# Scores of three attention blocks: 64-row products per head, or 128-row products with q's two parts stacked

## The chip, the cores and the metric

The kernel runs on one core of a Trainium2 chip. Its time is the device time of one execution in microseconds, median of several executions on the same chip. The engines that matter here are TensorE (PE in the rows, PEld for its weight loads), VectorE (DVE), ScalarE (ACT), GpSimd (POOL, which here only issues DMAs), and SyncE (SP, which issues the loads of weights).

## What is computed

Two transformer blocks are applied to x of 512 tokens by 1024 features, all in float32. The parts that the change touches are three attention blocks. In the first block a windowed attention (a, 8 heads of 64, 2 heads of k and v, window 128) and a neighbourhood attention (b, 8 heads, each with its own k and v) are computed from the same normalised input; in each layer of the second block there is one sliding-window attention (c, 8 heads of q, 2 of k and v). Cut to what matters:

```python
sc = jnp.einsum('bqkgd,bskd->bkgqs', qi, ki).astype(jnp.float32) * scale
sc = sc - slopes[:, :, None, None] * dist.astype(jnp.float32)
sc = jnp.where(valid, sc, -jnp.inf)
p = jax.nn.softmax(jnp.concatenate([sc, sink_col], axis=-1), axis=-1)[..., :-1]
return jnp.einsum('bkgqs,bskd->bqkgd', p.astype(v.dtype), vi)
```

Around them stand the products with w_in, the gates, w_proj and w_out, and the feed-forward layers with w_up, w_down and the gated pairs, which take most of the time.

## The kernel before, in words

Activations are kept transposed, features on partitions and 512 tokens along the free axis. Each float32 operand is held as two float32r tiles, a high part (a rounded copy, made by ScalarE) and a low part (the rest, made by VectorE), and each product is three matmuls: high by high, high by low, low by high. The tiles live in 52 slots of 128 by 512 (`slot[i]`, named r in the rows); `take` and `give` hand them out.

`Tile.mm` (lines 460 to 462) makes a product of a weight block with the activations, 24 matmuls of 512 columns for 1024 features. Weights come through `raw` and are split by line 386 (ScalarE) and line 388 (VectorE), five half-blocks ahead of their use.

The products for q, k and v end in an evacuation: `scaled` (lines 863 and 865; `scaled_by_columns`, line 871, for b) multiplies by the norm's factor `inv` on VectorE into a tile `evs`, and `split_act` (lines 566 and 567) makes the high part on ScalarE and the low part on VectorE, each 128 by 512. One such tile holds two heads, head g = 0 on partitions 0 to 63 and g = 1 on 64 to 127.

An attention block is a list of steps, one for a pair of heads c and a block of 128 queries i: 16 steps each for a and b, in one run, and 16 for c in each layer. A step has four stages. `qk` makes the scores (line 734, tiles sa, sb, sc): for each of the two heads three matmuls that contract over the head's 64 partitions, over 256 or 384 keys; then VectorE adds the bias and takes the maximum (line 739) and the negated maximum (lines 744 to 749). `soft` takes the exponentials on ScalarE (lines 755 and 758) and returns `rest`, the division by the sum on VectorE (lines 763 to 766). `tr` transposes the probabilities on TensorE (line 775, tiles pt) and splits them (lines 566 and 567). `pv_` multiplies with v (line 795, tiles ya, yb, yc; 128 rows, 256 columns), and `y_plain` evacuates the result (lines 903 and 904) in two halves of 64 partitions.

`run_attention` writes out the order of the work by hand. It goes through turns s; in each it issues `qk` of step s, then fillers (the products for later q, k, v, gates and so on, in the order of the tables FILL_AB and FILL_C, in portions of six matmuls) up to the middle of the turn, then `pv_` and `tr` of earlier steps, then `soft` of step s, two weight splits, `rest`, and fillers again. `tr` comes one turn after `soft` in a and b and two turns after in c. With `head=1` two filler portions (12 matmuls) stand ahead of the first scores. What is issued is executed in that order on each engine. `ev_v` defers the transposes of v (tile vtr) to the end of a later product.

Tables of bias for b (bb) are loaded by DMAs that GpSimd issues; SyncE's queue carries the weights.

## Time and profile before

| | us |
|---|---|
| median of 3 runs (2461.2 to 2463.68) | 2461.51 |
| the profiled execution | 2462.84 |
| its span | 2461.0 |
| TensorE busy | 2438.8 (99%) |
| VectorE busy | 1959.3 (80%) |
| ScalarE busy | 1261.1 (51%) |
| GpSimd busy | 11.6 (0%) |
| attention a and b in the span | about 31 to 263 |
| attention c of each layer | about 1085 to 1190 and 1950 to 2055 |

The profile's page is read from above: busy time of each engine, the chain of work that ended last, and the groups of instructions by line. A matmul's recorded duration includes the way through the array, so two matmuls in a row overlap in the rows; what one costs is the distance from its start to the next one's start.

### The profile page before, as it was taken

How to read it: one execution, taken by the hardware profiler on the slowest of the kernel's cores; microseconds unless marked ns; L12 is line 12 of the kernel's file. 1: busy time of each engine (PE TensorE's matmuls, PEld its weight loads, DVE VectorE, ACT ScalarE, POOL GpSimd, SP SyncE). 2: the span in 40 equal slices, each digit the busy share in tenths (PEclk: the TensorE clock that was granted, in tenths of full speed). 3: DMA queues.
4: the chain of work that ended last, by engine and by line, in shares of the span. 5: the costliest groups of instructions: out<-in, count | busy, mean ns of one | idle time of the engine just before them, and what ended most of it. 6: DMA issues, size and time to landing. Idle time of an engine off the chain costs nothing.

```text
span 2461.0 us, 39533 instructions
## 1 busy us (share of the span) xinstructions
PE 2438.8 (99%) x15118; PEld 2171.3 (88%) x15118; DVE 1959.3 (80%) x3950; ACT 1261.1 (51%) x2744; POOL 11.6 (0%) x26
## 2 busy tenths in 40 slices
PE   9999999999999999999999999999999999999998
PEld 7888888999879999988899999899999878999997
DVE  7778578877689878768798888898887687988885
ACT  5554355544465545544565445665445454654454
POOL 0000000000000000000000000000000000000000
PEclk9999999999999999999999999999999999999999
DMA  4222332333323332322223333323333322233322
GB/s 162 70 93 90 121 108 82 101 95 103 105 83 99 96 112 87 114 95 69 86 82 99 108 98 102 103 93 110 99 104 107 102 69 77 75 107 107 107 94 80
DMA packets 74621, 239.45 MB, mean 97 GB/s; under 512 B 8768, under 2 KB 10816, under 8 KB 74432
## 3 DMA queue, kind: packets, MB, share of 16 engines
q1 hardware_dynamic: 71248, 228.49, 29.3%
q0 software_dynamic: 1600, 6.82, 1.0%
q8 instruction: 118, 1.93, 0.3%
q10 hardware_dynamic: 1584, 1.64, 0.2%
q14 instruction: 71, 0.58, 0.1%
HBM read 234.81 MB, written 2.10 MB: 96 GB/s over the span
## 4 chain that ended last, share of the span: by engine, by line
PE 93%; DVE 5%; ACT 1%; issue 0%; DMA 0%; ACTq 0%; DVEq 0%
PE X L1114 7%; PE X L1112 7%; PE X L1113 7%; PE YZ L1112 5%; PE YZ L1113 5%; PE YZ L1114 5%; PE mlp_D L460 2%; PE mlp_D L461 2%; PE mlp_D L462 2%; PE 1, 'ffn1'_D L460 2%; PE 0, 'ffn2'_D L460 2%; PE 0, 'ffn1'_D L460 2%; PE 0, 'ffn2'_D L461 2%; PE 0, 'ffn1'_D L461 2%; PE 1, 'ffn1'_D L461 2%; PE 0, 'ffn1'_D L462 2%
## 5 line engine op out<-in xcount | busy, mean ns | idle before, releaser
L388 DVE TENSOR_TENSOR wl<-raw,wh 128x512 fp32r<-128x512 f32 (+2 forms) x890 | 531.8, 609 | 96.0 <-ACT wh L386 89.1
L386 ACT CAST wh<-raw 128x512 fp32r<-128x512 f32 (+2 forms) x890 | 469.8, 556 | 5.3 <-PE 0, 'ffn2'_D L461 1.0
L1112 PE MATMUL X<-r,wh 128*128 128x256 f32 x1568 | 445.2, 284 | 3.8 <-ACT g L1118 3.6
L1114 PE MATMUL X<-r,wl 128*128 128x256 f32 x1568 | 444.1, 283 | 0.0
L1113 PE MATMUL X<-r,wh 128*128 128x256 f32 x1568 | 443.9, 283 | 0.0
L386 ACT CAST wh<-s 128x512 fp32r<-128x512 f32 x392 | 242.6, 620 | 224.0 <-DVE s L365 218.7
L1112 PE MATMUL YZ<-r,wh 128*128 128x256 f32 x1176 | 334.2, 284 | 0.8 <-ACT u L1124 0.8
L1113 PE MATMUL YZ<-r,wh 128*128 128x256 f32 x1176 | 333.2, 283 | 0.0
L1114 PE MATMUL YZ<-r,wl 128*128 128x256 f32 x1176 | 333.1, 283 | 0.0
L388 DVE TENSOR_TENSOR wl<-s,wh 128x512 fp32r<-128x512 f32 x392 | 268.9, 686 | 69.2 <-ACT wh L386 67.4
L1112 PEld LDWEIGHTS X<-r,wh 128*128 128x128 f32 x1568 | 300.2, 191 | 15.2 <-ACT g L1118 4.0
L1113 PEld LDWEIGHTS X<-r,wh 128*128 128x128 f32 x1568 | 300.2, 191 | 10.3 <-issue 1.2
L1114 PEld LDWEIGHTS X<-r,wl 128*128 128x128 f32 x1568 | 300.3, 192 | 0.0
L1112 PEld LDWEIGHTS YZ<-r,wh 128*128 128x128 f32 x1176 | 226.2, 192 | 1.6 <-ACT u L1124 1.4
L1113 PEld LDWEIGHTS YZ<-r,wh 128*128 128x128 f32 x1176 | 226.1, 192 | 0.2 <-issue 0.2
L1114 PEld LDWEIGHTS YZ<-r,wl 128*128 128x128 f32 x1176 | 226.1, 192 | 0.0
L1126 ACT COPY g<-X 128x256 f32<-128x256 f32 x98 | 36.5, 372 | 141.6 <-PE X L1114 141.4
L1127 DVE TENSOR_TENSOR u<-u,g 128x256 f32<-128x256 f32 x98 | 41.6, 425 | 75.8 <-ACT g L1126 75.8
L460 PE MATMUL mlp_D<-r,wh 128*128 128x512 f32 x256 | 100.1, 391 | 0.0
L461 PE MATMUL mlp_D<-r,wh 128*128 128x512 f32 x256 | 100.1, 391 | 0.0
L462 PE MATMUL mlp_D<-r,wl 128*128 128x512 f32 x256 | 99.6, 389 | 0.0
L1122 ACT COPY u<-X 128x256 f32<-128x256 f32 x98 | 36.5, 373 | 101.0 <-PE X L1114 101.0
(426 smaller groups left out, 5251.2 us busy)
## 6 DMA issues: line engine op xcount, KB each, us to landing
raw<-in_w SPq DMA_DIRECT2D x318, 512.0 KB, 3.7
raw<-in_w SPq DMA_DIRECT2D x64, 384.0 KB, 3.4
raw<-in_w SPq DMA_DIRECT2D x32, 448.0 KB, 3.7
raw<-in_w SPq DMA_DIRECT2D x32, 320.0 KB, 2.9
raw<-in_w SPq DMA_DIRECT2D x32, 256.0 KB, 2.7
bb<-in_rpb POOLq DMA_DIRECT2D x12, 384.0 KB, 3.5
xt<-in_x POOLq DMA_DIRECT2D x8, 256.0 KB, 2.9
xt<-in_x SPq DMA_DIRECT2D x2, 512.0 KB, 6.3
```

Source lines behind the costliest of these rows:

```text
L386: nc.scalar.copy(h[:, :w], src)
L388: nc.vector.tensor_tensor(lo[:, :w], src, h[:, :w].bitcast(F32), ALU.subtract)
L460: nc.tensor.matmul(self.ps, h[:, c], hx, start=(self.n == 1), stop=False)
L461: nc.tensor.matmul(self.ps, h[:, c], lx, start=False, stop=False)
L462: nc.tensor.matmul(self.ps, lo[:, c], hx, start=False, stop=end)
L1112: nc.tensor.matmul(out, h[:, c], hx, start=first, stop=False, skip_group_check=skip)
L1113: nc.tensor.matmul(out, h[:, c], lx, start=False, stop=False, skip_group_check=skip)
L1114: nc.tensor.matmul(out, l[:, c], hx, start=False, stop=(k == 3), skip_group_check=skip)
L1122: nc.scalar.copy(u[:, lo], out)
L1126: nc.scalar.copy(g[:, hi], out)
L1127: nc.vector.tensor_tensor(u[:, hi], u[:, hi], g[:, hi], ALU.add)
```

## The change

The scores of a head are now made over all 128 partitions. For each head g a slot holds q's high part in the head's own 64 partitions and q's low part in the other 64. For k there are two slots for each head: one with k's high part in both halves, one with its low part in both. A score is then two matmuls, the stacked q with each of the two; together they also contain the product of the two low parts. `ev_q` and `ev_k` take the place of `ev_split`: the high and low parts are made by operations of 64 partitions each, and what has to stand in the other half is copied there by DMAs that GpSimd issues (`move`), two for each q and four for each k, of 64 by 512 elements. k takes four slots in place of two. k's product now stands ahead of q's at the head of each attention block and for each pair in FILL_AB, where the kb and qb entries also come earlier, and `head=2` puts 24 filler matmuls ahead of the first scores. In `run_attention` the exponentials (`soft`) are issued ahead of `pv_` and `tr`; `rest` stays where it was. In `y_plain` both high copies come ahead of both low parts.

```diff
-MIX1_HEAD = [("qa", 0), ("ka",), ("va",)]
+MIX1_HEAD = [("ka",), ("qa", 0), ("va",)]
...
             for g in range(2):
-                r = slice(HD * g, HD * g + HD)
-                qs = slice(P * i, P * i + P)
-                for j, (a, b) in enumerate(((qh, kh), (qh, kl), (ql, kh))):
-                    nc.tensor.matmul(sp[:, g, :w], a[r, qs], b[r, sl], start=(j == 0), stop=(j == 2))
+                qg, kg = slot[q(c)[g]], k(c)[2 * g:2 * g + 2]
+                for j in range(2):
+                    nc.tensor.matmul(sp[:, g, :w], qg[:, P * i:P * i + P], slot[kg[j]][:, sl], start=(j == 0), stop=(j == 1))
...
-    def run_attention(steps, fillers, needs, head=1, late=False):
+    def run_attention(steps, fillers, needs, head=2, late=False):
...
             fill_to((s + MID) / slots, SLACK[0])
+            if s < n:
+                rest = steps[s][1](steps[s][4])
             if s > lag:
                 k = s - lag - 1
                 steps[k][3](steps[k][4])
             if lag <= s < n + lag:
                 steps[s - lag][2](steps[s - lag][4])
             if s < n:
-                rest = steps[s][1](steps[s][4])
                 split_to(st["next"] + 2)
                 rest()
...
+    def rows(g):
+
+        return slice(HD * g, HD * g + HD)
+
+    def move(out, g_out, src, g_src):
+        nc.gpsimd.dma_start(out.bitcast(F32)[rows(g_out), :], src[rows(g_src), :])
+
+    def ev_q(ids, turn=scaled):
+
         def f(ps):
-            split_act(turn(ps, "evs", scale), slot[ids[0]], slot[ids[1]])
+            t = turn(ps, "evs", QS)
+            for g in range(2):
+                nc.scalar.copy(slot[ids[g]][rows(g), :], t[rows(g), :])
+            for g in range(2):
+                nc.vector.tensor_tensor(t[rows(g), :], t[rows(g), :], slot[ids[g]][rows(g), :].bitcast(F32), ALU.subtract)
+            for g in range(2):
+                move(slot[ids[g]], 1 - g, t, g)
+        return f
+
+    def ev_k(ids, turn=scaled):
+
+        def f(ps):
+            t = turn(ps, "evs")
+            for g in range(2):
+                nc.scalar.copy(slot[ids[2 * g]][rows(g), :], t[rows(g), :])
+            for g in range(2):
+                hi, lo = slot[ids[2 * g]], slot[ids[2 * g + 1]]
+                nc.vector.tensor_tensor(lo[rows(g), :], t[rows(g), :], hi[rows(g), :].bitcast(F32), ALU.subtract)
+            for j in range(2):
+                for g in range(2):
+                    i = ids[2 * g + j]
+                    move(slot[i], 1 - g, slot[i].bitcast(F32), g)
         return f
...
             for g in range(2):
                 r = slice(HD * g, HD * g + HD)
+                nc.scalar.copy(hi[r, cs].rearrange("p (a q) -> p a q", a=2), yp[r, :, g, :])
+            for g in range(2):
+                r = slice(HD * g, HD * g + HD)
                 src = yp[r, :, g, :]
-                nc.scalar.copy(hi[r, cs].rearrange("p (a q) -> p a q", a=2), src)
```

The order on the engines moves at three places. First, TensorE at the first scores of block a. Before (qa_388 is the product for the second pair of heads; after the arrow stand the streamed k, then the loaded q):

```order
L461 MATMUL qa_388<-r_95,wh_268 128x512
L462 MATMUL qa_388<-r_94,wl_269 128x512
L734 MATMUL sa_407<-r_106,r_104 128x256
L734 MATMUL sa_407<-r_107,r_104 128x256
L734 MATMUL sa_407<-r_106,r_105 128x256
```

The same three names follow for the second head, on the other 64 partitions, and then the second half of qa_388. After (qa_398 is the same product, vtr the transposes of v, qa_462 the next product):

```order
L462 MATMUL qa_398<-r_102,wl_322 128x512
L915 MATMUL vtr<-ident,evv 128x128 x4
L731 MATMUL sa_440<-r_106,r_104 128x256
L731 MATMUL sa_440<-r_107,r_104 128x256
L731 MATMUL sa_440<-r_108,r_105 128x256
L731 MATMUL sa_440<-r_109,r_105 128x256
L460 MATMUL qa_462<-r_88,wh_327 128x512
```

Six matmuls have become four, and all of qa_398 and the four transposes now stand ahead of them.

Second, ScalarE in a turn of block a. Before (ya is a product with v, pta the transposes of probabilities, mxa and ta the maxima and scores of the turn's own step, wh a weight split):

```order
L903 CAST r_116<-ya_557 64x256 x2
L566 CAST r_138<-pta_639 128x768
L755 ACTIVATE mxa_605<-mxa_605 128x2
L758 ACTIVATE ta_604,dena_649<-ta_604,mxa_605 128x256 x2
L386 CAST wh_662<-raw_335 128x512
```

After, in the same turn:

```order
L386 CAST wh_642<-raw_335 128x512
L752 ACTIVATE mxa_637<-mxa_637 128x2
L755 ACTIVATE ta_636,dena_653<-ta_636,mxa_637 128x256 x2
L929 CAST r_116<-ya_592 64x256 x2
L566 CAST r_138<-pta_669 128x768
```

The exponentials have moved ahead of the evacuations of the product and of the transposes.

Third, GpSimd ahead of the first scores of block b. Before (bb are the bias tables; nothing but the making of `ident` stands on this queue ahead of them):

```order
L945 MEMSET ident 128x128
L946 ISA
L946 AFFINE_SELECT ident<-ident 128x128
L1022 DMA bb_1545<-in_rpb 128x768
L1022 DMA bb_1549<-in_rpb 128x768
L1022 DMA bb_1621<-in_rpb 128x768
```

After (r_118 to r_129 are the slots of the second pair's k, r_130 one of its q's):

```order
L879 DMA r_118<-r_118 64x512
L879 DMA r_128<-r_128 64x512
L879 DMA r_119<-r_119 64x512
L879 DMA r_129<-r_129 64x512
L1051 DMA bb_1556<-in_rpb 128x768
L1051 DMA bb_1560<-in_rpb 128x768
L879 DMA r_130<-evs 64x512
```

The loads of the bias tables now stand behind the moves of k in GpSimd's queue.

## Rows read from the trace of the kernel before

**Rows 1.** Page, chain that ended last, share of the span by engine

```profile
PE 93%; DVE 5%; ACT 1%; issue 0%; DMA 0%; ACTq 0%; DVEq 0%
```

**Rows 2.** Busy time by stretch; columns: stretch, length, then busy (count) by engine

```profile
28.00:138.00 110.00, 109.27 (x605) 88.03 (x606) 83.89 (x239) 55.73 (x143) 1.21 (x2) 1.00 0.22 68
138.00:260.00 122.00, 121.46 (x678) 98.69 (x677) 96.13 (x251) 60.24 (x155) 5.37 (x10) 1.00 0.29 90
1080.00:1190.00 110.00, 110.00 (x592) 88.26 (x592) 87.97 (x264) 55.02 (x154) 0.00 (x0) 1.00 0.25 73
```

**Rows 3.** Timeline of PE, a score block of 256 keys; columns: start, duration, instruction

```profile
57.02 0.39 PE L462 MATMUL ga<-r,wl 128*128 128x512 f32 x1
57.34 0.62 PE L734 MATMUL sa<-r,r 64*128 64x256 f32 x6
...
58.23 0.40 PE L461 MATMUL ga<-r,wh 128*128 128x512 f32 x1
```

**Rows 4.** The same, only what runs at 57.36 to 57.45

```profile
57.34 0.39 PE L734 MATMUL sa<-r,r 64*128 64x256 f32 x2
```

**Rows 5.** The same view, a score block of 384 keys

```profile
37.06 0.40 PE L462 MATMUL qa<-r,wl 128*128 128x512 f32 x1
37.38 0.80 PE L734 MATMUL sa<-r,r 64*128 64x384 f32 x6
...
38.45 0.39 PE L461 MATMUL qa<-r,wh 128*128 128x512 f32 x1
```

**Rows 6.** The same view, a product with v in block a, 128 rows

```profile
59.18 0.39 PE L462 MATMUL ga<-r,wl 128*128 128x512 f32 x1
59.40 1.24 PE L795 MATMUL ya<-r,r 128*128 128x256 f32 x9
60.48 0.60 PE L775 MATMUL pta<-ident,ta 128*128 128x128 f32 x4
```

**Rows 7.** Timeline, all engines, start of block a

```profile
27.94 0.69 DVE L865 SCALAR_TENSOR_TENSOR evs<-qa,inv 128x512 f32<-128x512 f32 x1 [1.90 <-ACT inv L703]
28.66 0.62 ACT L566 CAST r<-evs 128x512 fp32r<-128x512 f32 x1 [0.76 <-DVE evs L865]
...
28.68 0.50 PE L460 MATMUL qa<-r,wh 128*128 128x512 f32 x1 [0.70 <-DVE evs L865]
...
31.61 1.05 PE L734 MATMUL sa<-r,r 64*128 64x256 f32 x6
```

**Rows 8.** DMA issues: count, KB each, median us from issue to landing

```profile
bb<-in_rpb POOLq DMA_DIRECT2D x12, 384.0 KB, 3.5
xt<-in_x POOLq DMA_DIRECT2D x8, 256.0 KB, 2.9
```

**Rows 9.** Groups by line: count | busy, mean ns | idle before, releaser

```profile
L1120 DVE TENSOR_TENSOR g<-YZ,g 128x256 f32<-128x256 f32 x98 | 40.8, 416 | 0.0
...
L904 DVE TENSOR_TENSOR r<-yc,r 64x256 fp32r<-64x256 f32 x32 | 13.5, 421 | 10.7 <-ACT r L903 10.3
```

**Rows 10.** Waits of VectorE, us 28 to 260; columns: total us, times, longest

```profile
DVE r L904 <- ACT r L903: 9.2, 17, 1.7
...
DVE dena L763 <- ACT ta L758: 5.2, 12, 0.6
```

**Rows 11.** The same, us 1080 to 1190

```profile
DVE r L904 <- ACT r L903: 4.4, 9, 1.0
DVE denc L763 <- ACT tc L758: 4.2, 11, 0.6
```

**Rows 12.** Waits of TensorE, us 28 to 260

```profile
PE qa L460 <- DVE evs L865: 0.7, 1, 0.7
```

**Rows 13.** Timeline, all engines, a late step of block a

```profile
129.36 0.75 DVE L766 TENSOR_SCALAR ta<-ta,dena 128x384 f32<-128x384 f32 x2
...
130.25 0.82 PE L775 MATMUL pta<-ident,ta 128*128 128x128 f32 x6
```

**Rows 14.** Timeline, all engines, start of block c

```profile
1078.64 0.59 ACT L703 COPY inv<-spread 128x512 f32<-128x512 f32 x1 [1.73 <-PE spread L691]
```

More of the change, by code (lines that the diff above doesn't have):

```diff
@@ L76 @@
 GB_ORDER += [("pb", 6), ("pb", 7)]
-MIX2_HEAD = [("q", 0), ("k",), ("v",)]
+MIX2_HEAD = [("k",), ("q", 0), ("v",)]
 FILL_C = [("q", 1), ("cc", 0), ("ch", 0), ("q", 2), ("cb", 0), ("cc", 1), ("ch", 1), ("q", 3), ("cc", 3),
@@ L725, in qk @@
             sp = bank(f"s{kind}{s}", True).rearrange("p (g k) -> p g k", g=2)
-            qh, ql = q(c)
-            kh, kl = k(c)
             w = max(n, 2 * P)
@@ L874, in scaled_by_columns @@
         return t
-    def ev_split(ids, scale=1.0, turn=scaled):
-        def f(ps):
-            split_act(turn(ps, "evs", scale), slot[ids[0]], slot[ids[1]])
+    def rows(g):
[3 more added lines that the diff above has]
+    def ev_q(ids, turn=scaled):
+        def f(ps):
+            t = turn(ps, "evs", QS)
[18 more added lines that the diff above has]
+                    move(slot[i], 1 - g, slot[i].bitcast(F32), g)
         return f
@@ L965, in two_blocks @@
     qa, ya, yb, qb, kb, vb = {0: take(2)}, {}, {}, {}, {}, {}
-    ka, va = take(2), take(2)
-    linear2(MIX1_HEAD, xop, [ev_split(qa[0], QS), ev_split(ka), ev_v(va)], ar, KC, make_inv, (5, 7))
+    ka, va = take(4), take(2)
+    linear2(MIX1_HEAD, xop, [ev_k(ka), ev_q(qa[0]), ev_v(va)], ar, KC, make_inv, (5, 7))
     ya_done = []
@@ L996, in make @@
                 return halves(key, [pair_of(ya[k]) for k in range(4)], ev_pa(key[1]))
-            ids = take(2)
+            ids = take(4 if key[0] == "kb" else 2)
             {"qa": qa, "qb": qb, "kb": kb, "vb": vb}[key[0]][key[1]] = ids
-            ev = {"qa": lambda: ev_split(ids, QS), "qb": lambda: ev_split(ids, QS, scaled_by_columns),
-                  "kb": lambda: ev_split(ids, 1.0, scaled_by_columns), "vb": lambda: ev_v(ids, scaled_by_columns)}
+            ev = {"qa": lambda: ev_q(ids), "qb": lambda: ev_q(ids, scaled_by_columns),
+                  "kb": lambda: ev_k(ids, scaled_by_columns), "vb": lambda: ev_v(ids, scaled_by_columns)}
             return halves(key, xop, ev[key[0]]())
@@ L1039, in rpb_bias @@
         return bt[:, :, P:] if i == 0 else bt
-    f_a = make_attention("a", ids_pair(qa), lambda c: pair_of(ka), lambda c: pair_of(va),
+    f_a = make_attention("a", qa.get, lambda c: ka, lambda c: pair_of(va),
                          y_plain(ya, lambda c: qa[c] + (ka + va if c == 3 else []), ya_done),
                          alibi("a", 0, 384), 0, (-1, 0, 1))
-    f_b = make_attention("b", ids_pair(qb), ids_pair(kb), ids_pair(vb),
+    f_b = make_attention("b", qb.get, kb.get, ids_pair(vb),
                          y_plain(yb, lambda c: qb[c] + kb[c] + vb[c]), rpb_bias, None, (-1, 0, 1))
@@ L1341, in mix2 @@
         qs, ys, tmp = {0: take(2)}, {}, {}
-        ks, vs = take(2), take(2)
-        linear2([(l,) + k for k in MIX2_HEAD], xop, [ev_split(qs[0], QS), ev_split(ks), ev_v(vs)], ar, 1, make_inv)
+        ks, vs = take(4), take(2)
+        linear2([(l,) + k for k in MIX2_HEAD], xop, [ev_k(ks), ev_q(qs[0]), ev_v(vs)], ar, 1, make_inv)
         cs = [take(2, late=True) for _ in range(4)]
@@ L1372, in make @@
                     qs[key[1]] = take(2)
-                    return halves((l,) + key, xop, ev_split(qs[key[1]], QS))
+                    return halves((l,) + key, xop, ev_q(qs[key[1]]))
                 return halves((l,) + key, xop, ev_conv(*key))
             return (key, 1.0, make)
-        f_c = make_attention(f"c{l}", ids_pair(qs), lambda c: pair_of(ks), lambda c: pair_of(vs),
+        f_c = make_attention(f"c{l}", qs.get, lambda c: ks, lambda c: pair_of(vs),
                              y_plain(ys, lambda c: qs[c] + (ks + vs if c == 3 else [])),
```

4 rows, old and new, of the table FILL_AB are left out of this document.

## The prediction

> **What bounds the kernel now.** I read the chain of waits first: 93% of the work that ended last is TensorE [rows 1]. Then the busy time by stretch over the three attention parts, the only places that the change reaches: TensorE is busy for 109.3 of 110 us and 121.5 of 122 in a and b, and for all of 110 in c [rows 2]; c comes once in each of two layers. TensorE waits for others almost nowhere: its largest wait in a and b is 0.7 us at the very start [rows 12]. So a TensorE slot that goes away shortens the run, as long as the engines beside it keep up. VectorE is the one to watch: busy for 83.9 + 96.1 = 180 of 232 us in a and b and for 88 of 110 in c [rows 2], and part of its idle time is waiting for ScalarE [rows 10, 11].
>
> **The scores, before.** Six matmuls look like six slots, but they aren't. A look at a moment inside the block shows two of them at once: the pair takes 0.39 us [rows 4], and all six with 256 keys end 0.62 us after the first started [rows 3]. Matmuls of the two heads stand on different halves of the partitions and run beside each other, so a block is three pairs. What it costs on TensorE is the distance between the neighbours on both sides. From the last matmul ahead (57.02) to the second one behind (58.23) are 1.21 us, in which two ordinary 512-column slots of 0.22 to 0.23 lie (59.18 to 59.40 in [rows 6] is one): 1.21 - 0.45 = 0.76 us. With 384 keys it is 38.45 - 37.06 - 0.45 = 0.94 us [rows 5].
>
> **The scores, after.** Four matmuls over 128 partitions, one behind the other. The price of one with 256 columns stands in the trace: nine products with v start at 59.40 and the next kind at 60.48, so 1.08 / 9 = 0.12 us each, and the matmul ahead of them has its ordinary slot, so such a block costs nothing at its edge [rows 6]. Four are 0.48 us, 0.28 less than before. No 384-column matmul over 128 partitions is in the trace; between 0.12 for 256 and 0.225 for 512 lies 0.17, so 0.69 for four and 0.25 less. In a and b half of the 32 steps have 256 keys and half 384; the 32 steps of c all stream 256. The saving is 48 x 0.28 + 16 x 0.25 = 13.4 + 4.0 = 17.4 us, all of it on the chain.
>
> The Trainium skill, TensorEngine Tiling (Array Packing), speaks against this: under Theoretical Speedup it gives matmuls that contract over 64 rows or fewer up to twice the rate when they run as separate tiles, and by that alone the six are worth three slots of 0.12 and the four cost 0.12 more, not 0.28 less. Its Key Properties add that a change of the tiling mode drains the engine; the 0.76 us against 3 x 0.12 in this trace agree, at 0.40 us a block.
>
> **The evacuations of q and k.** There are 16 tiles of q and 7 of k. Each had one high copy and one low subtraction of 128 partitions, and now has two of each with 64. Half the partitions save no time on VectorE: 64x256 takes 421 ns and 128x256 takes 416 [rows 9]. So each tile adds one more operation on each engine, 0.69 us at most on VectorE and 0.62 on ScalarE (the evacuation in [rows 7]): 23 x 0.69 = 15.9 us and 23 x 0.62 = 14.3 us, of which VectorE gets 9.0 in a and b (13 tiles) and 3.5 in each c (5 tiles). Both are beside TensorE, whose weights are split five half-blocks ahead. If VectorE had no room, they would count in full; that is the first rival. I take 1 us for single waits, with 0 and the rival's loss as ends.
>
> **The moves.** There are 2 x 16 + 4 x 7 = 60 DMAs of 128 KB from GpSimd's queue. The trace has 384 KB from that queue at 3.5 us to landing and 256 KB at 2.9 [rows 8]; one step further down is 2.3. No copy within the chip's on-chip memory is in the trace, so I keep ends one step lower, 1.7, and twice as long, 4.6. Scores that read a moved half wait for it, and TensorE is in order, so the fillers behind them wait too. For all but the first q and k of each part the order has the product end at least some fifty 512-column slots, 12 us, ahead of its first scores; evacuation and move take about 7. The first ones are closer.
>
> In a, the factor is ready at 27.94 [rows 7]. Then come on VectorE and ScalarE in turn: k scaled 0.69, ScalarE's copy 0.62, two subtractions 1.38, q scaled 0.69, copy 0.62, two subtractions 1.38: 27.94 + 5.4 = 33.3 us, and the last move lands near 35.7. TensorE meanwhile has the whole next product of q, 24 x 0.227 from 28.68, which is 34.2, and v's transposes, to 34.6. It waits 1.1 us, and the two score matmuls that need only the earlier move fit in: about 1.0 us (0.3 to 3.3 by the ends). The first scores of before took 1.05 us rather than 0.62 there [rows 7], which I don't credit. In c the factor is ready 1078.64 + 0.59 = 1079.2 [rows 14], but 15 matmuls of v are still to come in place of 3, so 12 x 0.23 = 2.8 us more cover than in a: no wait.
>
> GpSimd's queue is in order, and b's first bias tables now stand behind the moves of the second k. Before, they were loaded long ahead. Now the table lands about 1.1 + 3.5 us after k's last subtraction [rows 8], and VectorE has some 4 us of other work up to its use: a wait of VectorE by 0 to 1 us, which TensorE sees only where its slack is gone. I take nothing.
>
> **The order of ScalarE and VectorE.** The exponentials stood behind the evacuations of v's product and of the transposes, which wait for TensorE; now they run as soon as the maxima are there. What VectorE waits for exponentials, 5.2 us for a's and 4.2 in each c [rows 10, 11], should mostly go, and with both high copies of y first, about half of its waits there (9.2 and 4.4 us). None of this is on TensorE's path by itself; it pays for the added 0.69s. It is needed: late in a the division ends at 129.36 + 0.75 = 130.11 and the transposes that read it start at 130.25 [rows 13].
>
> **The sum.** -17.4 + 1.0 (start of a) + 1.0 (single waits) = -15.4 us. The profiled execution took 2462.84 with a span of 2461.0, so it would become 2447.4; it lies 1.3 above the median, and from the median 2461.5 the forecast is 2446.1 us, 0.6% faster.
>
> **The rivals.**
> VectorE takes over in the attention parts. Its busy time there grows by 15.9 us. If its waits stayed as they are, attention would grow by that and the gain of TensorE would be lost: 2461.5 + 15.9 + 1 = 2478, slower. It decides from the point where the waits that go are worth less than what is added. By the rows, a's exponentials (5.2), as much again for b's (taken alike), c's (2 x 4.2) and half of y's (9.2 + 2 x 4.4 = 18, so 9) are some 28 us, more than 15.9: even with VectorE as the bound the parts would shrink by 12, which gives 2451 with the start. For it: the 0.14 us above. Against it: the largest wait of TensorE in all of a and b is the 0.7 us at the start [rows 12]. Relieved (2449 to 2456) 0.2, unrelieved 0.04.
>
> What a block costs beyond its matmuls stays. Three pairs at 0.12 are 0.36, so that is 0.76 - 0.36 = 0.40 us. If it belongs to the waits and the change of operands and not to the halves, four slots cost 0.48 + 0.40 = 0.88: 0.12 more for 48 blocks and 0.17 for 16, 8.5 us, and 2461.5 + 8.5 + 2 = 2472, slower. Against it: nine products with v cost 1.08 with nothing at the edge [rows 6]. 0.04.
>
> The moves land late. If each needs 4.6 us rather than 2.3, the start of a loses 2.3 more and each c 0.6, what its 2.8 us of cover don't hide behind the 1.1 and the 2.3: 2446.1 + 3.5 = 2449.6. The Trainium skill, SBUF — State Buffer, in its section SBUF: two separate sides, says that GpSimd can't write a DMA's descriptors while VectorE runs an operation on both ports, and gives about 620 ns that became 3100. Such a delay of 2.5 us at each of three starts would give 2453. Against it, the median landings of that queue are 2.9 and 3.5 us [rows 8], for tables that land while VectorE is busy for four fifths of the time. 0.08 for either.
>
> The change doesn't do what it says, because something that I don't see keeps TensorE waiting at each block for the moved halves: within 5 us of before, 0.04.
>
> **How the numbers follow.** Forecast 0.60, VectorE relieved 0.2, late moves 0.08, nothing gained 0.04, slower 0.08 for the two rivals. The range runs from 2443 (17.4 saved and nothing lost but 1) to 2456, the upper end of the relieved rival. 0.2% is 4.9 us, about what a measurement here can tell from no change, so faster begins at 2456.6: faster 0.87, same 0.05, slower 0.08.
>
> **What would show it.** In the profile after: the score line with four matmuls of 128 rows at 0.12 and 0.17 us, ordinary slots on both sides, and attention parts shorter by some 8 us (a with b) and 4.4 (each c). The start of a has one wait of TensorE for a DMA, of about 1 us. VectorE's busy time there is up by 9 and 3.5 us, and its waits at the division and the low parts of y are down. The prediction is wrong if TensorE waits for VectorE or ScalarE at the transposes or the products with v in many turns, or if later scores wait for moves.

## The result: 1.2% slower

The changed kernel takes 2491.57 us (median of 4 runs, 2491.07 to 2492.03) against 2461.36 for the kernel before; the ratio is 1.0122, 95% interval 1.0109 to 1.0134. The forecast was 2446.1, so the sign is wrong and 45 us are to be explained. The profiled execution took 2491.07 with a span of 2489.3.

The chain that ended last, where [rows 1] had TensorE at 93%:

```profile
PE 77%; DVE 12%; ACT 5%; issue 4%; DMA 0%; POOL 0%; ACTq 0%; DVEq 0%; POOLq 0%
```

Busy time by stretch of the profile after, columns as in [rows 2] (c begins 18 us later here, so its stretch is moved):

```profile
28.00:138.00 110.00, 103.04 (x525) 85.81 (x526) 79.77 (x221) 56.74 (x141) 9.41 (x18) 0.98 0.26 79
138.00:263.00 125.00, 117.76 (x626) 98.14 (x626) 99.47 (x260) 63.72 (x159) 16.01 (x30) 1.00 0.37 113
1098.00:1208.00 110.00, 104.75 (x530) 86.84 (x529) 86.43 (x262) 55.06 (x155) 4.12 (x8) 0.97 0.27 80
```

TensorE now stands idle for 7.0, 7.2 and 5.3 us, where it had 0.7, 0.5 and none. VectorE is busy for 0.73, 0.80 and 0.79 of these stretches, against 0.76, 0.79 and 0.80 before: it isn't an engine that is full that holds TensorE up, but engines that wait for each other. The idle times understate the loss: a matmul of 512 columns is on record for 0.39 us and the next one starts after 0.23, so a wait of up to 0.16 us doesn't show as idle; and where the granted clock (third column from the end) is below 1.00, busy time is longer too. What TensorE waits for in a and b, where [rows 12] has the single row (total us, times, longest):

```profile
PE ya L792 <- DVE r L933: 2.7, 2, 2.0
PE ya L792 <- ACT r L566: 2.2, 3, 1.5
PE pta L772 <- DVE ta L763: 2.1, 6, 0.9
PE sb L731 <- DVE r L567: 2.1, 2, 1.7
...
PE sa L731 <- DMA r<-evs: 0.8, 2, 0.4
```

Most of the waits lie at the transposes and the products with v, which the prediction had named as the sign of its failure. What changed most is where ScalarE waits. These are two of its rows in a and b, us 28 to 263:

```profile
ACT tb L755 <- DVE mxb L741: 30.0, 10, 4.4
...
ACT mxa L752 <- DVE mxa L746: 18.3, 6, 3.7
```

Line 752 (755 in the kernel before) begins the exponentials of a, line 755 (758) those of b; they need the maxima from VectorE. In the kernel before the same two waits are 1.3 and 1.2 us:

```profile
ACT tb L758 <- DVE mxb L744: 1.3, 2, 0.7
ACT mxa L755 <- DVE mxa L749: 1.2, 1, 1.2
```

In c of the first layer it is the same, 20.3 us after (us 1098 to 1215) and 2.5 before (us 1080 to 1193):

```profile
ACT mxc L752 <- DVE mxc L746: 20.3, 8, 3.0
...
ACT mxc L755 <- DVE mxc L749: 2.5, 3, 1.5
```

A turn of block a shows what 48 us of such waiting do (start, duration, instruction; idle time ahead and who ended it):

```profile
80.74 1.00 PE L772 MATMUL pta<-ident,ta 128*128 128x128 f32 x6 [0.31 <-DVE ta L763]
81.44 0.55 DVE L736 CUSTOM_DVE_ANT_0 ta<-sa,ala 128x384 f32<-128x384 f32 x1
...
82.71 0.16 DVE L746 TENSOR_TENSOR mxa<-mxa,snk 128x2 f32<-128x2 f32 x1
...
82.90 0.20 ACT L752 ACTIVATE mxa<-mxa 128x2 f32<-128x2 f32 x1 [2.99 <-DVE mxa L746]
...
83.01 0.60 ACT L755 ACTIVATE ta<-ta,mxa 128x384 f32<-128x384 f32 x1
...
84.83 0.78 ACT L566 CAST r<-pta 128x768 fp32r<-128x768 f32 x1
...
85.64 0.96 DVE L567 TENSOR_TENSOR r<-pta,r 128x768 fp32r<-128x768 f32 x1 [1.57 <-ACT r L566]
...
88.17 0.41 DVE L736 CUSTOM_DVE_ANT_0 ta<-sa,ala 128x256 f32<-128x256 f32 x1
...
89.36 0.20 ACT L752 ACTIVATE mxa<-mxa 128x2 f32<-128x2 f32 x1 [3.23 <-DVE mxa L746]
```

The transposes of an older step end at 81.74. ScalarE is idle and could copy them out, but it takes its work in order, and at its head stand the exponentials, which wait until 82.90. So the copy starts at 84.83, 3.1 us late (1.2 us of it ScalarE is idle, the rest goes to the exponentials and a gate that stand ahead); VectorE, also in order, waits 1.57 for it, divides, and reaches the next scores at 88.17 only (their matmuls had ended at 84.97); so ScalarE waits 3.23 for the next maxima. ScalarE and VectorE hand the work to and fro in series, 6.46 us from exponentials to exponentials.

A turn of the kernel before has the same work side by side:

```profile
74.27 0.82 PE L775 MATMUL pta<-ident,ta 128*128 128x128 f32 x6
74.34 0.16 DVE L749 TENSOR_TENSOR mxa<-mxa,snk 128x2 f32<-128x2 f32 x1
...
76.18 0.79 ACT L566 CAST r<-pta 128x768 fp32r<-128x768 f32 x1
...
76.98 0.61 ACT L758 ACTIVATE ta<-ta,mxa 128x384 f32<-128x384 f32 x1
77.01 0.96 DVE L567 TENSOR_TENSOR r<-pta,r 128x768 fp32r<-128x768 f32 x1
```

The maxima (74.50) and the transposes (75.09) come ready at nearly the same time. ScalarE takes the transposes' copy first, so VectorE's subtraction from 77.01 runs beside the exponentials from 76.98. With the exponentials first, VectorE has to wait for them, and ScalarE afterwards for VectorE's subtraction, division and next maxima.

The scores themselves became what was forecast. In this timeline the 256-key block ends in an ordinary slot, 54.91 - 54.44 = 0.47 us for four matmuls (forecast 0.48):

```profile
54.21 0.39 PE L462 MATMUL ga<-r,wl 128*128 128x512 f32 x1
54.44 0.64 PE L731 MATMUL sa<-r,r 128*128 128x256 f32 x4
54.91 0.40 PE L460 MATMUL ga<-r,wh 128*128 128x512 f32 x1
```

### The profile page after: what moved, and what is told of

Read it like the earlier page. It is cut to its first block, busy times and chain, and to the rows that moved or that the text cites. A ratio compares the mean times of both kernels' runs of the same rounds, so it can differ in the third digit from the quotient of the medians.

```text
span 2489.3 us, 39529 instructions
## 1 busy us (share of the span) xinstructions
PE 2442.1 (98%) x14990; PEld 2185.8 (88%) x14990; DVE 1973.9 (79%) x3973; ACT 1277.1 (51%) x2767; POOL 42.9 (2%) x86
## 4 chain that ended last, share of the span: by engine, by line
PE 77%; DVE 12%; ACT 5%; issue 4%; DMA 0%; POOL 0%; ACTq 0%; DVEq 0%; POOLq 0%
PE X L1143 7%; PE X L1142 7%; PE X L1141 7%; PE YZ L1141 5%; PE YZ L1143 5%; PE YZ L1142 5%; DVE wl L388 2%; PE mlp_D L461 2%; PE mlp_D L460 2%; PE mlp_D L462 2%; PE 1, 'ffn1'_D L460 2%; PE 0, 'ffn2'_D L460 2%; PE 0, 'ffn1'_D L460 2%; PE 0, 'ffn2'_D L461 2%; PE 0, 'ffn1'_D L461 2%
## 5 line engine op out<-in xcount | busy, mean ns | idle before, releaser
L1141 PEld LDWEIGHTS X<-r,wh 128*128 128x128 f32 x1568 | 300.7, 192 | 14.8 <-ACT g L1147 4.0
```

The source lines that it names most:

```text
L1141: nc.tensor.matmul(out, h[:, c], hx, start=first, stop=False, skip_group_check=skip)
```

## The experiments

Each was timed beside the kernel before, whose medians lie between 2461.1 and 2462.2; a difference between two kernels of the table is good to about 1 us. e3, e8, e9 and e10 leave parts of the scores out, n0, n2, a0 and a1 the low parts of weights, so their output isn't the reference's. To locate the time I use, beside the median, two stretches of the profiled execution: a with b, from the first `spread` matmul to the first of b's projection, and one c, from v's first matmul to the first of its projection. The rest of the span, with c of the second layer taken out too, lies between 1982.7 and 1986.3 us in all runs. c of the second layer agrees with the first within 0.6 us, except in a0 (117.2).

| kernel | median us | ratio, 95% interval | a with b | c (first layer) |
|---|---|---|---|---|
| before | 2461.4 | | 239.3 | 117.9 |
| after | 2491.6 | 1.0109 to 1.0134 | 255.0 | 124.8 |
| e1_exp_late | 2456.4 | 0.9967 to 0.9986 | 238.2 | 115.5 |
| e2_exp_early_alone | 2476.1 | 1.0044 to 1.0074 | 250.1 | 119.9 |
| e5_exp_between | 2483.3 | 1.0074 to 1.0104 | 256.6 | 120.3 |
| n0_less_vector | 2461.5 | 0.9989 to 1.0008 | 238.6 | 117.9 |
| n2_less_vector_exp_early | 2461.4 | 0.9989 to 1.0008 | 238.5 | 117.9 |
| a0_after_less_vector | 2467.4 | 1.0014 to 1.0034 | 243.8 | 119.7 |
| a1_late_less_vector | 2455.8 | 0.9969 to 0.9988 | 237.1 | 115.8 |
| e3_scores_alone | 2449.0 | 0.9930 to 0.9963 | 234.2 | 114.1 |
| e8_halves_alone | 2468.1 | 1.0017 to 1.0037 | 244.5 | 117.8 |
| e9_halves_y_order | 2449.9 | 0.9938 to 0.9967 | 235.1 | 114.4 |
| e4_y_interleaved | 2495.9 | 1.0123 to 1.0153 | 258.8 | 125.5 |
| e10_halves_new_order | 2453.9 | 0.9957 to 0.9980 | 236.9 | 115.4 |
| e7_head_one | 2465.1 | 1.0006 to 1.0026 | 244.7 | 116.3 |
| f3_old_fill | 2465.8 | 1.0008 to 1.0026 | 249.0 | 115.4 |
| f1_fewer_vector_ops | 2479.6 | 1.0057 to 1.0087 | 252.5 | 118.7 |
| f2_q_one_subtraction | 2455.9 | 0.9967 to 0.9985 | 238.4 | 115.4 |
| f4, f2 with f3 | 2466.4 | 1.0012 to 1.0030 | 248.4 | 115.4 |

**Where the exponentials stand.** Theory A: their place in mid-turn makes ScalarE wait for late maxima and costs the whole 30 us and more. The rival: the moves or VectorE's added subtractions do. e1 undoes the place alone, e2 makes it alone, e5 goes halfway.

```diff
--- after.py
+++ e1
-            if s < n:
-                rest = steps[s][1](steps[s][4])
             if s > lag:
                 k = s - lag - 1
                 steps[k][3](steps[k][4])
             if lag <= s < n + lag:
                 steps[s - lag][2](steps[s - lag][4])
             if s < n:
+                rest = steps[s][1](steps[s][4])
                 split_to(st["next"] + 2)
```

> The changed kernel with one thing undone: the exponentials stand behind the evacuations of v's product and of the transposes again. Theory A (exponentials in mid-turn make ScalarE wait for VectorE's maxima, and the transposes' evacuation behind them comes late): most of the loss goes, 2446 to 2456 us, and TensorE's waits for ScalarE and VectorE in the attention parts fall under 3 us. Theory B (VectorE has no room for the added subtractions of q and k): 2480 to 2492 us, little changed. Theory C (the moves and their landings): little changed as well.

> The kernel before with one thing of the change alone: the exponentials in mid-turn, ahead of the evacuations. Theory A: slower by most of the 30 us, 2475 to 2492 us, with ScalarE waiting 15 us or more for the maxima in a and b. Theories B and C: within 5 us of 2461, or a little faster.

e1 takes 2456.4: the place alone costs 35.2 us, more than all that was lost. By stretch these are 16.8 us in a with b and 9.3 in each c. In the kernel before (e2, the same lines moved the other way) it costs 14.8. In e1 ScalarE waits for the maxima for 1.8 and 1.4 us instead of 18.3 and 30.0, and TensorE in a and b for ScalarE and VectorE for 4.9 instead of 13.3 (under 3 was expected). The same evacuations run beside the exponentials:

```profile
80.91 0.78 ACT L566 CAST r<-pta 128x768 fp32r<-128x768 f32 x1
81.59 0.20 ACT L752 ACTIVATE mxa<-mxa 128x2 f32<-128x2 f32 x1
...
81.72 0.96 DVE L567 TENSOR_TENSOR r<-pta,r 128x768 fp32r<-128x768 f32 x1 [1.48 <-ACT r L566]
...
85.03 0.80 ACT L566 CAST r<-pta 128x768 fp32r<-128x768 f32 x1 [0.26 <-PE pta L772]
...
85.89 0.20 ACT L752 ACTIVATE mxa<-mxa 128x2 f32<-128x2 f32 x1
```

The copy at 85.03 comes 0.04 us after its transposes end, and this turn takes 4.30 us from exponentials to exponentials. Turns differ; over the 16 steps of a, from the first `sa` matmul to the first `sb`, the mean is 106.2 / 16 = 6.6 us in e1 and 116.5 / 16 = 7.3 after.

e5 puts the exponentials behind the evacuation of v's product and ahead of that of the transposes:

```diff
--- after.py
+++ e5
-            if s < n:
-                rest = steps[s][1](steps[s][4])
             if s > lag:
                 k = s - lag - 1
                 steps[k][3](steps[k][4])
+            if s < n:
+                rest = steps[s][1](steps[s][4])
             if lag <= s < n + lag:
```

> The changed kernel with the exponentials one place later: behind the evacuation of v's product, still ahead of that of the transposes. Theory A1 (what costs is the transposes' evacuation waiting behind the exponentials): little of the loss goes, 2480 to 2495 us. Theory A2 (what costs is y's evacuation waiting): most of it goes, 2455 to 2465 us.

It takes 2483.3, so, undone in this order, 8 of the 35 us hang on v's product and 27 on the transposes: the loop through the division. By stretch the 8 us all lie in c (4.5 in the first layer, as much in the second); a with b, at 256.6, gains nothing. And it gains nothing although ScalarE's waits for the maxima there fall from 30.0 and 18.3 to 15.1 and 11.9: the length of these waits isn't what they cost. Why v's product matters in c alone wasn't followed.

**Does the place cost for itself, or because VectorE is late?** n0 and n2 take work from VectorE: in the attention parts the weights' low parts are no longer made.

```diff
--- before.py
+++ n0
+        attn = key[0] in ("qa", "ka", "va", ...) or key[1] in ("q", "k", "v", "cb", "cc", "ch")
-        lo = wt_p.tile([P, S], F32R, tag="wl", name=f"wl{idx}")
+        lo = h if attn else wt_p.tile([P, S], F32R, tag="wl", name=f"wl{idx}")
...
-        nc.vector.tensor_tensor(lo[:, :w], src, h[:, :w].bitcast(F32), ALU.subtract)
+        if not attn:
+            nc.vector.tensor_tensor(lo[:, :w], src, h[:, :w].bitcast(F32), ALU.subtract)
```

> The kernel before, without the low parts of the weights in the attention parts: line 388 is left out there and the third matmul of each product reads the high part again, so the products there are rougher and TensorE's work is the same. It is the base for the next run. All theories: TensorE is the bound, so 2458 to 2462 us.

> The run before it with the exponentials in mid-turn; the weights' low parts are left out in the attention parts in the same way. Theory A in full (the early place hurts because VectorE's maxima come late, as it runs behind TensorE): with VectorE relieved the maxima come in time, so within 3 us of the run before it. Rival E (the early place costs by itself, whatever VectorE has to do): slower than the run before it by 10 to 15 us, as with the full work (2476 against 2462).

n0 changes nothing, as TensorE set the end. n2, with the exponentials early besides, takes 2461.4 as well: the 14.8 us of e2 are gone. ScalarE still waits 25.0 and 11.0 us for maxima there, but TensorE waits for nobody in a and b except the 0.7 us at the start:

```profile
ACT tb L760 <- DVE mxb L746: 25.0, 10, 4.3
...
ACT mxa L757 <- DVE mxa L751: 11.0, 5, 3.0
...
PE qa L462 <- DVE evs L868: 0.7, 1, 0.7
```

It is the room on VectorE that decides whether such a wait costs anything.

The same in the changed kernel, with the exponentials early (a0) and late (a1):

> The changed kernel whole, exponentials in mid-turn, but without the weights' low parts in the attention parts (the high part stands in for the low one in the products, so TensorE does the same work; the output is rougher than the reference's). VectorE loses one subtraction of 128x512 for each of these weights. Theory A (the early exponentials cost only because VectorE runs behind, so that the maxima that they wait for are late): nearly all of the 30 us goes, and what is left is the gain of the scores less the moves and y's new order, 2447 to 2454 us. Rival (the place in mid-turn, the fill list or the moves cost for themselves): 2465 us or more.

> a0 (the changed kernel without the weights' low parts in the attention parts; the output is rougher than the reference's) with the exponentials behind the evacuations of v's products and transposes. Theory A (with VectorE ahead the place of the exponentials costs nothing inside the blocks; a0's excess is the waits for the moves at the starts and the lower clock behind them): the same as a0 within 4 us, 2463 to 2471 us. Rival (the early exponentials cost for themselves in the changed kernel): 2450 to 2457 us, like the changed kernel with late exponentials (2456.4) or better.

Both runs come out in the ranges of the rivals, and yet neither theory holds whole. The early place costs 35.2 us with VectorE's full work and 2467.4 - 2455.8 = 11.7 without: two thirds of the loss are VectorE's lateness, one third stays. In much of a, a0 runs as theory A has it: TensorE is busy for all of 10 us in each slice from 40 to 110. What it loses beyond a1 is 6.7 us in a with b and 3.9 and 1.9 in the two c. Around the start of b these are single waits: 2.3 us once where a product with v waits for a transposes' evacuation (a1: 0.7), and a granted clock below full behind it. In each c a product with v waits 1.2 us for VectorE, which it doesn't in a1. a0's slices around the start of b:

```profile
150.00:160.00 10.00, 7.70 (x37) 6.17 (x38) 6.24 (x18) 4.36 (x10) 2.15 (x4) 0.93 0.40 134
160.00:170.00 10.00, 10.00 (x50) 8.56 (x50) 6.33 (x18) 6.51 (x16) 0.55 (x1) 0.90 0.45 160
```

The same slices of a1 have 8.90 and 10.00 us at a clock of 1.00. The profiled a1 is one of its shortest runs (2452.6), 14.1 us below that of a0, and 2.0 of these lie ahead of the attention; so this split is good to a few us. At the start of a both wait longer for q's moves than the changed kernel does, 2.9 us (a0) and 3.2 (a1) against 0.8; as both do, the difference doesn't rest on it.

**The scores and the halves.** e3 has the four 128-row matmuls from unstacked parts and nothing else of the change; e8 adds the halves, e9 y's new order to these.

```diff
--- before.py
+++ e3
-                r = slice(HD * g, HD * g + HD)
                 qs = slice(P * i, P * i + P)
-                for j, (a, b) in enumerate(((qh, kh), (qh, kl), (ql, kh))):
-                    nc.tensor.matmul(sp[:, g, :w], a[r, qs], b[r, sl], start=(j == 0), stop=(j == 2))
+                for j, (a, b) in enumerate(((qh, kh), (ql, kl))):
+                    nc.tensor.matmul(sp[:, g, :w], a[:, qs], b[:, sl], start=(j == 0), stop=(j == 1))
```

> The kernel before with the scores alone as two matmuls over all 128 partitions for each head. Both heads' features are then contracted together and the stacked parts aren't there, so the scores are not the reference's; everything else is as before. All theories: the term of the sum for the score blocks, 17.4 us less, 2444 us, if VectorE and ScalarE have room for attention parts that are shorter by that much; up to 2450 if they have not.

2449.0: 12.4 us of the forecast 17.4. By stretch it is 5.1 of 8.5 in a with b and 3.8 of 4.5 in each c. TensorE's idle time in the three stretches of [rows 2] is 1.23, 1.35 and 0.64 us, up by 0.5, 0.8 and 0.64 from 0.73, 0.54 and 0, and its waits are mostly for VectorE, so part of the rest is a VectorE that no longer quite keeps up:

```profile
28.00:138.00 110.00, 108.77 (x590) 93.74 (x589) 84.45 (x242) 56.70 (x146) 1.75 (x3) 1.00 0.24 71
138.00:260.00 122.00, 120.65 (x659) 104.17 (x659) 97.13 (x253) 60.55 (x156) 4.82 (x9) 1.00 0.29 90
1080.00:1190.00 110.00, 109.36 (x575) 92.74 (x573) 88.13 (x264) 53.53 (x154) 0.00 (x0) 1.00 0.25 77
```

```diff
--- e3
+++ e8
-            split_act(turn(ps, "evs", scale), slot[ids[0]], slot[ids[1]])
+            t = turn(ps, "evs", scale)
+            hi, lo = slot[ids[0]], slot[ids[1]]
+            rows = [slice(HD * g, HD * g + HD) for g in range(2)]
+            for r in rows:
+                nc.scalar.copy(hi[r, :], t[r, :])
+            for r in rows:
+                nc.vector.tensor_tensor(lo[r, :], t[r, :], hi[r, :].bitcast(F32), ALU.subtract)
```

> The kernel before with the scores over 128 partitions (unstacked, so not the reference's scores) and q's and k's high and low parts made by two operations of 64 partitions each, without the moves, and with the old order of everything else. Theory B' (the added operations on VectorE and ScalarE are what is left between 2449 and 2456): 2453 to 2457 us. Rival (the waits for moves, the longer head and the new filler order are what is left): 2449 to 2451 us.

2468.1, above both ranges: 19.2 us for 15.9 us of VectorE's work, as if none were hidden. I took that for the price of the halves until e9, which differs only in y's evacuation:

```diff
--- e8
+++ e9
             for g in range(2):
                 r = slice(HD * g, HD * g + HD)
+                nc.scalar.copy(hi[r, cs].rearrange("p (a q) -> p a q", a=2), yp[r, :, g, :])
+            for g in range(2):
+                r = slice(HD * g, HD * g + HD)
                 src = yp[r, :, g, :]
-                nc.scalar.copy(hi[r, cs].rearrange("p (a q) -> p a q", a=2), src)
                 nc.vector.tensor_tensor(lo[r, cs].rearrange("p (a q) -> p a q", a=2), src,
```

> The kernel before with unstacked scores of 128 rows, q's and k's parts made by two instructions of 64 partitions each, no moves, and of the three new orders only y's: both copies of its high parts ahead of both subtractions. Its output is not the reference's. The same with y's copies and subtractions in turn took 2468.1 us. If y's order is worth here what it was worth in the changed kernel (4.4 us), 2462.5 to 2465 us; if it is the whole recovery, 2455 to 2458 us; if the order of the fill list is all of it, 2467 to 2469 us.

2449.9, below all three ranges. Without one instruction less, 18.2 us are back, and the halves with y's new order cost about 1 us; what that order would bring without the halves no run shows. In e8 ScalarE's second copy of y is released by VectorE's first subtraction, and whatever is queued behind it on ScalarE waits too (the second row is e3, which has y's old order without the halves):

```profile
ACT r L908 <- DVE r L909: 17.2, 15, 3.2
...
ACT r L902 <- DVE r L903: 15.4, 16, 2.0
```

In e9 the copies wait for TensorE's product alone (12.1 and 1.6 us in a and b), when there is nothing to copy yet:

```profile
ACT r L907 <- PE yb L794: 12.1, 6, 2.9
```

That y's order decides is shown by e9; the rows alone don't show it, since e3 has nearly as much of this wait and is as fast as e9. I read it as the fault of the exponentials in another place: ScalarE's queue headed by an instruction that waits for VectorE, which costs where the halves leave VectorE no room. e4 undoes y's order in the changed kernel:

> The changed kernel with y's two high copies and two low parts interleaved again (copy, subtraction, copy, subtraction). Theories A, B and C: within 5 us of 2491, either way. A rival D, that both copies ahead hold the transposes' evacuation back: 2480 us or less.

2495.9, 4.4 us worse than after. That y's order saves less here than in e9 would fit a ScalarE that the exponentials already hold up, but no run shows it.

**The lists and the moves.** e10 is e9 with the other orders of the change (k ahead of q, the new fill list, two pieces ahead of the first step), still without moves. The step from e10 to e1 is then the stacked placing with its 60 moves.

> The kernel before with scores as two products of 128 rows from unstacked parts, q's and k's parts made by two instructions of 64 partitions each, no moves, and in addition the three orders of the changed kernel: y's copies ahead of its subtractions, k ahead of q in the heads and the fill list, and two pieces of filler ahead of the first step. It leaves out the product of the two heads' proper parts, so its output is not the reference's. The same with the old orders took 2468.1 us, the changed kernel with late exponentials, which has the moves besides, 2456.4 us. If the moves cost nothing and the new orders are what brings the 12 us, it takes 2455 to 2458 us. If the moves cost several us too, 2449 to 2453 us. If the new orders bring only what y's order brought in the changed kernel (4.4 us), 2462 to 2465 us, and something in the stacked form itself is cheaper than the halves.

2453.9: the lists cost 4.0 us (1.8 in a with b, 1.0 in each c), the moves with the stacking 2.5 (e1 2456.4). The lists are needed with the moves, though. e7 takes the second piece ahead of the first step away from e1, f3 its fill list:

> The changed kernel with late exponentials and one piece of filler ahead of the first step instead of two. If the second piece only covers the landing of the moves (2.3 us) at three starts, 2456 to 2460 us against 2456.4 us; if it does more than that, namely leaves the exponentials more room in the first steps, over 2461 us; if it covers nothing, since TensorE waited 1.1 us at the start of a in spite of it, 2455.5 to 2457.5 us. The output is the reference's.

> The changed kernel with late exponentials and the fill list of the kernel before for a and b (q of b ahead of its k, pieces of y's projection where they stood); two pieces ahead of the first step as in the changed kernel. The output is the reference's. Without moves the old orders were 4.0 us faster than the new ones (2449.9 against 2453.9 us): if that holds with the moves, 2451.5 to 2454 us; if the new list covers the landing of k's moves ahead of b's scores, which the old one doesn't, 2457 to 2465 us.

Both are worse by about 9 us. In f3 v's transposes in b wait 5.1 us for v's scaling on VectorE, and in the slice from 160 to 170 the granted clock is 0.69. In e7 the same transposes wait 4.5 us and the clock there is 0.66. And in both, scores wait for moves. In e7 TensorE waits 3.7 us for q's at the start of a, where the clock is 0.83 (30 to 40), and 2.2 and 2.4 at the starts of the two c. In f3 the four moves of one k of b are issued at 233.06 and land from 235.25 to 237.59, and its scores wait 3.8 us in all. TensorE's rows in a and b of f3:

```profile
PE sb L731 <- issue: 2.3, 1, 2.3
PE sb L731 <- DMA r<-r: 1.8, 3, 1.2
```

So the new list and the second piece do cover the moves, as they were meant to.

f1, f2 and f4 try to make e1 better with fewer subtractions: one of 128 partitions for both heads, the rest by copies and moves.

```diff
--- e1
+++ f2 (f1 has the like for k, with five moves, two of which overwrite what others read)
-            for g in range(2):
-                nc.scalar.copy(slot[ids[g]][rows(g), :], t[rows(g), :])
-            for g in range(2):
-                nc.vector.tensor_tensor(t[rows(g), :], t[rows(g), :], slot[ids[g]][rows(g), :].bitcast(F32), ALU.subtract)
-            for g in range(2):
+            nc.scalar.copy(slot[ids[0]], t)
+            nc.scalar.copy(slot[ids[1]][rows(1), :], slot[ids[0]].bitcast(F32)[rows(1), :])
+            nc.vector.tensor_tensor(t, t, slot[ids[0]].bitcast(F32), ALU.subtract)
+            for g in (1, 0):
                 move(slot[ids[g]], 1 - g, t, g)
```

> The changed kernel with the exponentials behind the evacuations of v's products and transposes, and with q's and k's parts made by fewer instructions: ScalarE copies all 128 partitions of the high part in one instruction and the second head's 64 partitions in another, VectorE makes the low part of both heads in one subtraction of 128 partitions where there were two of 64, and DMAs do the rest of the placing (two moves for each q as now, five for each k instead of four). The output is the reference's. Theory A (what is lost between the 2449.0 us of the unstacked scores alone and the 2456.4 us of the stacked kernel with late exponentials is VectorE's added subtractions): VectorE is back at the count of the kernel before in q and k, and 5 to 7 of the 7.5 us return, 2449 to 2452 us. Rival (the loss is the landing of the moves, or the order in which things are written): no better, 2455 to 2460 us, since the fifth move of k lands 2.3 us behind the others.

2479.6, far above both ranges: 23 us worse with less work for VectorE. Two of k's five moves must wait for others to land, and q's moves stand behind them in GpSimd's queue:

```profile
38.40 0.52 POOL L878 DMA_DIRECT2D r<-r  x1 [4.90 <-DMA r<-r]
38.91 1.03 POOL L878 DMA_DIRECT2D r<-evs  x2
...
42.22 1.19 PE L731 MATMUL sa<-r,r 128*128 128x256 f32 x4 [7.90 <-DMA r<-evs]
```

TensorE waits 7.90 us at the start of a, and 3.8 and 4.2 at the starts of the two c. In b it waits 7.1 more once: there a load of the bias tables stands behind k's last move in the same queue, VectorE waits 8.4 us for the table, and TensorE for VectorE. Together these are 23 us. f2 leaves k as it was:

> The changed kernel with late exponentials, with q's low parts of both heads made by one subtraction of 128 partitions instead of two of 64, and k's parts as in the changed kernel, four moves without a chain. The output is the reference's. VectorE has 16 subtractions of 0.69 us less. If these are what keeps it from the 2449.9 us of the unstacked halves: 2450 to 2454 us. If the moves or the fill list keep it there: 2455 to 2457.5 us. If what cost 23 us in f1 was q's new form and not k's chain of moves in GpSimd's queue: over 2465 us.

> f2 and f3 together: q's low parts by one subtraction, and the old fill list, exponentials late. The output is the reference's. If both keep what they may bring, 2448 to 2451 us, the lowest of all that compute the reference; if the two share one cause, namely room on VectorE, 2450 to 2454 us; if the old list leaves k's moves uncovered, over 2456 us.

f2 takes 2455.9, the same as e1: sixteen subtractions less bring nothing, so once the exponentials stand late it isn't these that keep the stacked kernel 6.5 us above e9; by e10 it is the lists and the moves. f4 shows again that the old list doesn't go with the moves. The best kernels that compute the reference are e1 and f2, 0.2% below the kernel before.

## Why the prediction was wrong, point by point

From medians, each step being the difference of two kernels:

| step | forecast us | measured us | from |
|---|---|---|---|
| score matmuls | -17.4 | -12.4 | e3 - before |
| halves, with y's new order | +1.0 | +1.0 | e9 - e3 |
| lists: k first, fill, two pieces | not costed | +4.0 | e10 - e9 |
| moves and stacking | +1.0 | +2.5 | e1 - e10 |
| exponentials in mid-turn | relief, 0 | +35.2 | after - e1 |
| sum | -15.4 | +30.2 | |

- **The step that failed is the one on the order of ScalarE and VectorE.** It said that the exponentials "run as soon as the maxima are there", that none of this is on TensorE's path by itself, and that the waits saved on VectorE pay for the added work; the place of the exponentials stands in the sum at nothing. It costs 35.2 us (after against e1). It asked who is released earlier, and never who stands behind the moved instructions: the copies of the transposes, with which VectorE goes on at once. In the turn of before shown above maxima and transposes came ready within 0.6 us of each other, so 1.2 us of exponentials put ahead of the copy are about as much waiting for VectorE, and what VectorE does late is the next maxima. With VectorE relieved the same place costs 11.7 us, and in the kernel before, relieved, nothing (n2). The waits at the division did go as forecast (5.2 us for a in [rows 10], 1.7 after), but those at the low parts rose: y's, 9.2 us in [rows 10], are 16.3.
- **The rival "VectorE takes over"** had the right sign and, at 2478, a good half of the loss, but the wrong mechanism: VectorE isn't busier per us than before. I held it to be relieved by the very edit that did the harm, and so gave its slower half 0.04. The prediction also read TensorE's few waits [rows 12] as room. They showed only that the order of before just fitted: late in a the division ended 0.14 us ahead of the transposes [rows 13], and that row, which I had quoted, was the better guide.
- **The price of a score block** was right (0.47 us against 0.48 forecast), its whole gain not: TensorE got 12.4 of 17.4, since the engines beside it didn't all follow. A block of 384 keys took 0.71 (0.69 forecast). The rival by which 0.40 us a block would stay falls with e3. The Trainium skill, TensorEngine Tiling (Array Packing), has "Up to 2×" under Theoretical Speedup; with the rate doubled in full the 64-row form would have been the faster one, and for blocks of six matmuls e3 shows that it isn't.
- **Half-partition operations** cost the 0.69 us each that was taken: 64x512 takes 687 ns in the profile after. That this is 1 us in all was right with y's new order (e9) and 18 us off without it (e8), so the hit is in part luck. The prediction credited y's order with waits saved, and not with deciding whether the added work is hidden.
- **The moves** landed after 2.3 and 2.6 us by the medians, as estimated, and the start of a waited 0.8 us for them. The rival of late moves doesn't come in for this kernel (it does in e7 and f3, which cover them less); nor does the delay of GpSimd's descriptors that the Trainium skill describes in SBUF — State Buffer, SBUF: two separate sides, show in these medians. Whether VectorE ran operations on both ports just then no run here shows.

```profile
r<-evs POOLq DMA_DIRECT2D x32, 128.0 KB, 2.3
r<-r POOLq DMA_DIRECT2D x28, 128.0 KB, 2.6
```

- **The lists** were read only for whether the moves are covered. They cost 4.0 us (e10 against e9), more than the moves with the stacking. That the fillers are shifted by a few slots against the evacuations is the likely cause; by which waits wasn't followed.

What stays open: why the early exponentials still cost about 12 us with VectorE relieved. a0 shows single waits with a lower clock behind them, but no run took these away one by one. And why the early place costs 35.2 us in the changed kernel and 14.8 in the one before: the shorter score blocks and the halves may both leave VectorE less room, but no run tells them apart.

## What to carry to other kernels

On an engine that works in order and serves two chains, put first what another engine goes on with; what is put first instead can make the two engines work in series where the other one has little room, and neither's busy share shows it. Before moving an instruction ahead, follow one turn in the timeline and ask what is then queued behind it and who waits for that. When a piece of added work seems to cost all of its time, change the order around it before believing that the engine is full.

## What the runs showed of the hardware

- Behind some waits of TensorE the granted clock fell, and the wait cost more than its length. In the profile after it waits 2.01 us, and matmuls of 512 columns soon behind that start 0.43 us apart (126.28, 126.71) where 0.23 is usual: the 1.2 GHz level instead of 2.4. It didn't fall behind every such wait: behind 2.16 us in e10 (at 43) and 2.34 us in a1 (at 1085) it stayed full. The rows of the profile after:

```profile
123.30 1.90 PE L792 MATMUL ya<-r,r 128*128 128x256 f32 x9 [2.01 <-DVE r L933]
...
126.28 0.63 PE L461 MATMUL ga<-r,wh 128*128 128x512 f32 x1
126.71 0.63 PE L462 MATMUL ga<-r,wl 128*128 128x512 f32 x1
```

The stretch around it, with the granted clock (0.83) in the third column from the end:

```profile
120.00:130.00 10.00, 7.99 (x35) 6.61 (x34) 7.11 (x22) 6.26 (x18) 1.60 (x4) 0.83 0.36 107
```

- Copies of 128 KB within on-chip memory land in 2.3 and 2.6 us from GpSimd's queue in the profile after (medians of q's and k's; 2.2 to 2.6 in all kernels that have them), while VectorE is busy for 73 to 80% of the attention parts. Single ones take up to 3.7 us there, and up to 5.8 in a1.
